# Ada units in rows of two, three and four between the weight units of a hybrid decoder layer

## Chip, core and metric

The kernel runs on one core of a Trainium2 chip. The time is device microseconds from launch to end; a run's profile also gives the span from the first to the last instruction. All times below are in microseconds unless a row says ns.

## What is computed

One decoder layer for 256 prompt rows and 8 x 4 sample rows (T = 288 rows together), model width 2048, feed-forward width 8192, all in float32:

```python
mod = jax.nn.silu(c) @ w_ada + b_ada            # 9 conditions, w_ada is 2048 x 12288
sh_m, sc_m, gt_m, sh_f, sc_f, gt_f = jnp.split(mod[:, None, :], 6, axis=-1)
h = rmsnorm(x, g_pre_mix) * (1 + sc_m) + sh_m
q, k, v, gu, gv = jnp.split(h @ w_in, SPLITS, axis=-1)
attn_out = attend(q, k, v)                       # sliding window, sinks, relative bias
gmlp_out, v_rows = gmlp_spatial_gate(jax.nn.gelu(gu), jax.nn.gelu(gv), ...)
merged = jnp.concatenate([rmsnorm(attn_out, g_attn_out), rmsnorm(gmlp_out, g_gmlp_out)], axis=-1)
x = x + gt_m * rmsnorm(merged @ w_out, g_post_mix)
h = rmsnorm(x, g_pre_ff) * (1 + sc_f) + sh_f
f = jnp.square(jax.nn.relu(h @ w_ff1)) @ w_ff2
x = x + gt_f * rmsnorm(f, g_post_ff)
```

## The kernel before

**Units.** Activations lie transposed: 16 tiles of 128 features by 288 rows. Weights come in units of 1 MB (128 x 2048 floats), loaded by SyncE's DMA queue into five buffers `raw`. A weight unit of W_out, f1 or f2 (class `Main`) yields 128 output features: its two halves are split into a rounded part `h` (cast on ScalarE, line 321) and a remainder `l` (subtraction on VectorE, line 322), and TensorE runs 48 matmuls of 288 columns (lines 336, 337, 340: h by xh, h by xl, l by xh). Then `evac` moves the sum out of PSUM.

An **Ada unit** (class `Ada`) is a quarter of a block of `w_ada` and is not split: four float32 matmuls of 512 columns (line 363; each stands as two instructions in the trace), whose weights are the 32 columns of `sc`, so each of the four fills another 32 columns of the array. Four units make a block. After the last, ScalarE copies the PSUM tile to an SBUF tile `adS` (line 367, two buffers). `ada_fin` then transposes it on TensorE (line 375, four transposes) and VectorE reduces and scales it into the modulation (lines 377 to 387). Blocks of kinds 2, 3 and 4 (`Gm`, `Bf`, `Af`; 48 units) are needed around the end of W_out and the start of f1, those of kind 5 (`Gf`; 16 units) only at the end of the last f2 pass.

**Stages, in order of time.** W_in with attention and gating; then W_out's first four output tiles in eight *slabs* of 0.5 MB (`SlabK`, line 924: each slab brings two of 16 feature tiles for four open PSUM tiles), among which stand the eight gates of the gating (lines 730 to 738), a sum over partitions (line 264) and the norm `rgate` that the last four slabs need; then W_out's other twelve output tiles as `Main` units (from 350 us); then `resid` (norm, residual add, second norm); f1's first six output tiles in eight slabs; and f1 and f2 in four passes of 16 and 16 units.

**What sets the order.** A list `items` is written by hand; `drive` walks it, loads four units ahead and splits one ahead. `na(n)` takes the next n Ada units, with a block's `ada_fin` as soon as its units are through. A tile scheduler then orders each engine's queue, with `high_priority` for the slabs, the attention pieces and `resid`; a queue is worked off in its order, so an instruction that waits holds up all that is behind it on its engine. Before, `NA_S` puts 1, 1, 1, 1, 1, 1, 2, 2 Ada units behind the eight slabs of W_out, `NA_O` one behind each W_out unit (two behind the last), eight (`NA_R`) stand behind `resid`, and f1 has one item of the list `adas2` (a unit or a block's transposes) behind each unit of its second pass and the start of its third. `gvout` (line 718) multiplies the gated rows by a gain on GpSimd for an output; it takes its tile from the two `adS` buffers.

Of the kernel before, what the change touches and what calls it, by code (L numbers as in the profile page):

```python
# [10 lines left out]
F32 = mybir.dt.float32  # L11
F32R = mybir.dt.float32r
AF = mybir.ActivationFunctionType
ALU = mybir.AluOpType
# [9 lines left out]
NS = NB * NT_S  # L24
T = NP + NS
# [3 lines left out]
NO = 4  # L29
# [16 lines left out]
NAFT = 4  # L46
NA_L = (0, 2, 1, 3, 3, 0, 2)
NA_A = (1, 1, 1, 1, 1, 1)
NA_O, NA_R = 13, 8
NA_S = (1, 1, 1, 1, 1, 1, 2, 2)  # L50

WID = {1: (1,), 2: (2,), 3: (1, 2), 4: (4,), 5: (1, 4), 6: (2, 4), 8: (4, 4)}

# [52 lines left out]
def build():  # L106
# [32 lines left out]
    with tile.TileContext(nc) as tc, ExitStack() as root:  # L139
        cp = root.enter_context(tc.tile_pool(name="cp", bufs=1))  # L140
# [5 lines left out]
        ap_ = mid.enter_context(tc.tile_pool(name="ap", bufs=1))  # L146
# [3 lines left out]
        V, S, PE, G = nc.vector, nc.scalar, nc.tensor, nc.gpsimd  # L150
# [148 lines left out]
        class Unit:  # L299
            src = None  # L300
            cols = 2 * HALF
            n = HALF
# [348 lines left out]
        gm = {}  # L651
# [65 lines left out]

        def gvout():
            for h in (0, 4):
                gr = cp.tile([128, 2, T], F32, name="adS", bufs=2).rearrange("p a b -> p (a b)")[:NS, :512]  # L720
                G.dma_start(gr, bass.AP(d_gain.tensor, h * 128, [[0, NS], [1, 512]]))
                G.tensor_tensor(gr, gr, gm["vGs"][:, h:h + 4].rearrange("p h c -> p (h c)"), ALU.mult)
                G.dma_start(o_g[:, h * 128:h * 128 + 512], gr)

        def gate(h):
# [31 lines left out]
        items = list(first)  # L757
# [38 lines left out]
        adas = []  # L796
# [3 lines left out]
        adas2 = []  # L800
# [4 lines left out]
        def na(n):  # L805
            out = []
            while adas and n > 0:
                it = adas.pop(0)
                out.append(it)
                n -= it.src is not None  # L810
            if adas and adas[0].src is None:
                out.append(adas.pop(0))
            return out
# [3 lines left out]
        def do(f, *a):  # L817
            def run():
                with tc.high_priority(offset=HP):
                    f(*a)  # L820
            items.append(Do(run))
# [108 lines left out]
        def slab_o(q):  # L930
            items.append(SlabK(d_woA[q], q, NO, pre_o, bo))
            items.extend(na(NA_S[q]))

        for q in range(4):
            slab_o(q)
            if q < 2:
                for h in range(4 * q, 4 * q + 4):
                    do(gate, h)
                    do(ssq_gate, h)
            if q == 2:  # L940
                do(rgate)
                do(gvout)
        for q in range(4, 8):
            slab_o(q)

        og = []

# [20 lines left out]
        def ev_bo():  # L968
            for n in range(NO):
                ev_o(n)(bo[n][:, :T])  # L970

        items.append(Do(ev_bo))
        for n in range(NO, 16):
            items.append(Main(d_woB[n - NO], xh, xl, ev_o(n)))
            items += na((n - NO + 1) * NA_O // (16 - NO) - (n - NO) * NA_O // (16 - NO))
        items += na(len([it for it in adas if it.src is not None]) - NA_R)

        def resid():
            r = norm_r(st["so"].result(), "r_o", 0.0)
# [66 lines left out]
        for c in range(4):  # L1046
            for j in range(16):
                if c == 0 and j < NF:
                    continue
                items.append(Main(d_f1B[c * 16 + j - NF], xh, xl, ev_f1(j)))  # L1050
                if c > 0 and adas2:
                    items.append(adas2.pop(0))
            for n in range(16):
                items.append(Main(d_f2[c, n], fh, fl, ev_f2(c, n)))

# [126 lines left out]
```

## Time and profile before

| | before |
|---|---|
| median of 3 runs (lowest, highest) | 1324.22 (1323.6, 1330.82) |
| the profiled execution | 1323.86 |
| its span, first to last instruction | 1322.1 |
| mean granted TensorE clock, share of full | 0.995 |
| TensorE matmul busy | 1291.5 (98%) |
| VectorE busy | 735.5 (56%) |
| ScalarE busy | 543.6 (41%) |
| GpSimd busy | 38.9 (3%) |
| DMA, mean over the span | 220 GB/s |

In the timeline rows the first number is the start, the second how long the engine is busy from the first start to the last end. Successive matmuls overlap, so what a piece of work costs is read from one start to the next, not from the busy time. A bracket names the idle time ahead of a row and what ended it.

### The profile page before, as it was taken

What the parts mean: (1) busy time and instruction counts of PE and PEld (TensorE: products, weight loads), DVE (VectorE), ACT (ScalarE), POOL (GpSimd) and SP (SyncE); (2) the same over time, 40 slices, a digit from 0 to 9 for tenths busy, and PEclk for the clock granted to TensorE, in tenths of its full rate; (3) what the DMA queues carried; (4) which work ended last, traced back from release to release, by engine and by line L of the source; (5) the groups of instructions that cost most, each with busy time, mean ns of one, the idle gap of its engine ahead of it and who ended that gap; (6) DMA issues with size and microseconds to landing.
All of it is one profiled execution on the core that took longest, in us unless ns stands there. A gap on an engine that the chain in (4) does not pass through costs nothing.

```text
span 1322.1 us, 23368 instructions
## 1 busy us (share of the span) xinstructions
PE 1291.5 (98%) x9770; PEld 1174.6 (89%) x9770; DVE 735.5 (56%) x1405; ACT 543.6 (41%) x873; POOL 38.9 (3%) x61
## 2 busy tenths in 40 slices
PE   6999999999999999999999999999999999999997
PEld 5789785767788699999998989999999999999996
DVE  5888676667744496543334444444554444555554
ACT  5323243575433265444344443334443334444331
POOL 0210001211000000000000000000000000000000
PEclk8999999999999999999999999999999999999999
DMA  9998977577987675544466765446444444454411
GB/s 357 337 325 313 334 284 249 204 278 255 384 319 258 275 271 189 177 169 161 160 223 239 268 234 187 171 171 232 166 176 165 160 160 164 169 178 160 159 65 72
DMA packets 46010, 291.40 MB, mean 220 GB/s; under 512 B 5834, under 2 KB 6410, under 8 KB 15056
## 3 DMA queue, kind: packets, MB, share of 16 engines
q1 hardware_dynamic: 43344, 284.26, 59.2%
q0 software_dynamic: 2416, 5.47, 1.8%
q8 instruction: 76, 1.25, 0.4%
q14 instruction: 30, 0.25, 0.0%
q10 hardware_dynamic: 144, 0.18, 0.0%
HBM read 287.18 MB, written 2.70 MB: 219 GB/s over the span
## 4 chain that ended last, share of the span: by engine, by line
PE 93%; DVE 4%; DMA 2%; ACT 1%; issue 0%; SPq 0%; DVEq 0%; ACTq 0%
PE ps L336 22%; PE ps L340 22%; PE ps L337 21%; PE ada L363 6%; PE ps L924 5%; PE ps L485 4%; PE ps L488 4%; PE ps L486 4%; PE ada L375 1%; DVE l L322 1%; PE ps L572 1%; DMA x<-xT 1%; PE ps L567 1%; DMA raw<-wada 1%; DMA raw<-win 0%; DVE acc L983 0%
## 5 line engine op out<-in xcount | busy, mean ns | idle before, releaser
L322 DVE TENSOR_TENSOR l<-raw,h 128x1024 fp32r<-128x1024 f32 (+3 forms) x368 | 417.6, 1141 | 345.7 <-ACT h L321 341.0
L321 ACT CAST h<-raw 128x1024 fp32r<-128x1024 f32 (+3 forms) x368 | 359.1, 984 | 571.0 <-PE ps L337 476.7
L336 PE MATMUL ps<-xh,h 128*128 128x288 f32 x1120 | 304.5, 299 | 0.9 <-ACT sq L1007 0.7
L337 PE MATMUL ps<-xl,h 128*128 128x288 f32 x1120 | 301.2, 295 | 0.0
L337 PE MATMUL ps<-fl,h 128*128 128x288 f32 x1024 | 276.9, 295 | 0.0
L336 PE MATMUL ps<-fh,h 128*128 128x288 f32 x1024 | 276.9, 298 | 0.0
L336 PEld LDWEIGHTS ps<-xh,h 128*128 128x128 f32 x1120 | 210.5, 188 | 23.8 <-ACT fh L1008 12.6
L337 PEld LDWEIGHTS ps<-xl,h 128*128 128x128 f32 x1120 | 211.6, 189 | 0.0
L336 PEld LDWEIGHTS ps<-fh,h 128*128 128x128 f32 x1024 | 193.0, 188 | 0.8 <-ACT fh L1008 0.8
L337 PEld LDWEIGHTS ps<-fl,h 128*128 128x128 f32 x1024 | 192.2, 188 | 0.0
L340 PE MATMUL ps<-xh,l 128*128 128x288 f32 x1120 | 171.9, 295 | 0.4 <-DVE l L322 0.4
L340 PE MATMUL ps<-fh,l 128*128 128x288 f32 x1024 | 157.3, 296 | 0.0
L340 PEld LDWEIGHTS ps<-xh,l 128*128 128x128 f32 x1120 | 156.1, 188 | 0.6 <-DVE l L322 0.6
L340 PEld LDWEIGHTS ps<-fh,l 128*128 128x128 f32 x1024 | 142.7, 188 | 0.0
L485 PE MATMUL ps<-xh,h 128*128 128x288 f32 x416 | 117.9, 307 | 2.9 <-DVE gv L497 2.0
L363 PE MATMUL ada<-raw,sc 128*32 128x512 f32 (+2 forms) x1088 | 109.1, 485 | 10.1 <-DMA raw<-wada 10.0
L486 PE MATMUL ps<-xl,h 128*128 128x288 f32 x416 | 117.2, 299 | 0.0
L485 PEld LDWEIGHTS ps<-xh,h 128*128 128x128 f32 x416 | 77.8, 190 | 17.2 <-issue 6.3
L488 PE MATMUL ps<-xh,l 128*128 128x288 f32 x416 | 86.7, 299 | 0.0
L486 PEld LDWEIGHTS ps<-xl,h 128*128 128x128 f32 x416 | 79.2, 191 | 2.6 <-issue 2.4
L488 PEld LDWEIGHTS ps<-xh,l 128*128 128x128 f32 x416 | 66.1, 190 | 1.1 <-issue 1.0
L363 PEld LDWEIGHTS ada<-raw,sc 128*32 128x32 f32 x1088 | 29.7, 113 | 39.5 <-issue 32.0
(255 smaller groups left out, 932.1 us busy)
## 6 DMA issues: line engine op xcount, KB each, us to landing
raw<-wada SPq DMA_DIRECT2D x96, 1024.0 KB, 6.8
raw<-f SPq DMA_DIRECT2D x64, 1024.0 KB, 4.8
raw<-f1B SPq DMA_DIRECT2D x58, 1024.0 KB, 4.8
raw<-woB SPq DMA_DIRECT2D x12, 1024.0 KB, 7.0
raw<-win SPq DMA_DIRECT2D x11, 1024.0 KB, 8.9
raw<-win SPq DMA_DIRECT2D x14, 640.0 KB, 5.1
raw<-f1A SPq DMA_DIRECT2D x8, 768.0 KB, 6.0
raw<-win SPq DMA_DIRECT2D x6, 768.0 KB, 5.9
```

Of the source, the lines that this page charges most:

```text
L321: S.copy(h, rw)
L322: V.tensor_tensor(l, rw, h.bitcast(F32), ALU.subtract)
L336: PE.matmul(ps, w, self.mh[:, k], start=k == 0, stop=False)
L337: PE.matmul(ps, w, self.ml[:, k], start=False, stop=False)
L340: PE.matmul(ps, l[:, kk * 128:kk * 128 + 128], self.mh[:, k], start=False, stop=k == 15)
L363: PE.matmul(ps[g:g + 32, :cw], sc[:, k], self.raws[:, kk * cw:kk * cw + cw], start=k < 4, stop=k >= KT - 4, skip_group_check=True)
L375: PE.transpose(pt[:, q * 128:q * 128 + 128], sb[:, q * 128:q * 128 + 128], ident)
L485: PE.matmul(ps, w, xh[:, k0 + kk], start=kk == 0, stop=False)
L486: PE.matmul(ps, w, xl[:, k0 + kk], start=False, stop=False)
L488: PE.matmul(ps, l[:, o_ + kk * 128:o_ + kk * 128 + 128], xh[:, k0 + kk], start=False, stop=kk == s - 1)
L567: PE.transpose(ps[:, to * 128:to * 128 + 128], L[:, hf, q * 128:q * 128 + 128], ident)
L924: PE.matmul(self.bk[n][:, :T], w[:, n * 128:n * 128 + 128], m[:, k], start=k == 0 and p_ == 0, stop=k == KT - 1 and p_ == 2)
```

## The change

Four things are done to the order of the work, and one to a tile.

- Slabs of W_out: Ada units 0, 2, 0, 2, 0, 2, 0, 2 behind the eight slabs, eight in all where there were ten.
- W_out's units: three Ada units behind every second one, fifteen in all where there were thirteen, and none behind the last one. Eight stay behind `resid`.
- f1: four Ada units behind the 4th, 8th, 12th and 16th unit of the second pass; the third pass has none.
- A new function `group` takes the units of a row; the transposes of a block that ends inside the row stand behind the row, those of a block that ends with the row stand behind the next row (`late`).
- `gvout` is asked for behind the sixth slab where it was behind the third, takes its tile from the buffers `bias`, and multiplies on VectorE.

```diff
-NA_O, NA_R = 13, 8
-NA_S = (1, 1, 1, 1, 1, 1, 2, 2)
+NA_O, NA_G = 3, 4
+NA_S = (0, 2, 0, 2, 0, 2, 0, 2)
...
-                gr = cp.tile([128, 2, T], F32, name="adS", bufs=2).rearrange("p a b -> p (a b)")[:NS, :512]
+                gr = ap_.tile([128, 2, 384], F32, name="bias", bufs=3).rearrange("p a b -> p (a b)")[:NS, :512]
                 G.dma_start(gr, bass.AP(d_gain.tensor, h * 128, [[0, NS], [1, 512]]))
-                G.tensor_tensor(gr, gr, gm["vGs"][:, h:h + 4].rearrange("p h c -> p (h c)"), ALU.mult)
+                V.tensor_tensor(gr, gr, gm["vGs"][:, h:h + 4].rearrange("p h c -> p (h c)"), ALU.mult)
...
+        late = []
+        def group(src, n):
+            out, ends = [], list(late)
+            late.clear()
+            while src and n:
+                it = src.pop(0)
+                if it.src is None:
+                    ends.append(it)
+                else:
+                    out.append(it)
+                    n -= 1
+            if src and src[0].src is None:
+                late.append(src.pop(0))
+            return out + ends
...
             items.append(Main(d_woB[n - NO], xh, xl, ev_o(n)))
-            items += na((n - NO + 1) * NA_O // (16 - NO) - (n - NO) * NA_O // (16 - NO))
-        items += na(len([it for it in adas if it.src is not None]) - NA_R)
+            if n % 2 and n < 15:
+                items += group(adas, NA_O)
+        items += late
+        late.clear()
...
                 items.append(Main(d_f1B[c * 16 + j - NF], xh, xl, ev_f1(j)))
-                if c > 0 and adas2:
-                    items.append(adas2.pop(0))
+                if c == 1 and j % NA_G == NA_G - 1:
+                    items += group(adas2, NA_G)
+                    if not adas2:
+                        items += group(adas2, 0)
```

What this makes of the queues is shown at three places. Names: `xh`, `xl` the two parts of the activations, `h`, `l` those of a weight unit, `raw` an unsplit unit, `ps` and `ada` PSUM tiles, `sqa` a sum of squares, `nr` and `mn` tiles of a norm, `gu` the gated rows.

TensorE in f1's second pass, the first Ada units of that pass, before:

```order
L337 MATMUL ps_7400<-xl_79,h_7336 128x288
L340 MATMUL ps_7400<-xh_78,l_7337 128x288 x8
L363 MATMUL ada_7465<-raw_7210,sc_95 32x512 x4
L336 MATMUL ps_7472<-xh_78,h_7392 128x288
L337 MATMUL ps_7472<-xl_79,h_7392 128x288
```

and now:

```order
L340 MATMUL ps_7587<-xh_78,l_7527 128x288 x8
L363 MATMUL ada_7652<-raw_7390,sc_95 32x512 x4
L363 MATMUL ada_7652<-raw_7455,sc_95 32x512 x4
L363 MATMUL ada_7652<-raw_7520,sc_95 32x512 x4
L363 MATMUL ada_7652<-raw_7585,sc_95 32x512 x4
L336 MATMUL ps_7687<-xh_78,h_7644 128x288
```

Four units of one block stand in a row where one stood. W_out's twelve units have five rows of three in the same manner, and one single unit inside the first of the twelve.

TensorE in W_out's slabs, around the sum over partitions that `rgate` needs, before:

```order
L924 MATMUL ps<-xh,h 128x288
L375 MATMUL ada<-small,adS 128x128 x4
L924 MATMUL ps<-xh,h 128x288 x3
L924 MATMUL ps<-xl,h 128x288 x2
L264 MATMUL ps<-sqa,ones_81 128x288
L924 MATMUL ps<-xl,h 128x288 x2
L924 MATMUL ps<-xh,l 128x288 x4
L363 MATMUL ada<-raw,sc 32x512 x12
L924 MATMUL ps<-xh,h 128x288 x4
```

and now:

```order
L924 MATMUL ps<-xl,h 128x288 x4
L363 MATMUL ada<-raw,sc 32x512
L924 MATMUL ps<-xh,l 128x288 x4
L264 MATMUL ps<-sqa,ones_81 128x288
L924 MATMUL ps<-xh,h 128x288 x4
L924 MATMUL ps<-xl,h 128x288 x4
L924 MATMUL ps<-xh,l 128x288 x4
L363 MATMUL ada<-raw,sc 32x512 x3
L375 MATMUL ada<-small,adS 128x128 x4
L363 MATMUL ada<-raw,sc 32x512 x8
L924 MATMUL ps<-xh,h 128x288 x4
```

The last row of each is the start of the fifth slab, which needs `rgate`. Between line 264 and it there were six slab matmuls and three units; now there are twelve slab matmuls, three quarters of a unit, a block's transposes and two units.

VectorE over the same norm, before:

```order
L224 TENSOR_SCALAR mn<-ps 128x288
L214 TENSOR_TENSOR mn<-nr 128x288
L215 SCALAR_TENSOR_TENSOR mn<-mn 128x288
L322 TENSOR_TENSOR l<-raw,h 128x512
L216 SCALAR_TENSOR_TENSOR nr<-mn,nr 128x288
L322 TENSOR_TENSOR l<-raw,h 128x512
L794 TENSOR_TENSOR nr<-nr 128x288
L891 SCALAR_TENSOR_TENSOR gu<-gu,small,nr 128x288 x3
```

and now:

```order
L722 TENSOR_TENSOR bias<-bias,vGs 32x512 x2
L322 TENSOR_TENSOR l<-raw,h 128x512
L224 TENSOR_SCALAR mn<-ps 128x288
L214 TENSOR_TENSOR mn<-nr 128x288
L322 TENSOR_TENSOR l<-raw,h 128x512
L215 SCALAR_TENSOR_TENSOR mn<-mn 128x288
L322 TENSOR_TENSOR l<-raw,h 128x512
L216 SCALAR_TENSOR_TENSOR nr<-mn,nr 128x288
L322 TENSOR_TENSOR l<-raw,h 128x512
L794 TENSOR_TENSOR nr<-nr 128x288
L377 TENSOR_REDUCE adm<-ada 128x36
L891 SCALAR_TENSOR_TENSOR gu<-gu,small,nr 128x288
```

Between line 214 and line 891 three subtractions and a block's reduction stand where two subtractions stood.

ScalarE in `resid`, from its first norm to the first tiles of f1, before:

```order
L166 ACTIVATE nr<-ps 128x288
L367 COPY adS<-ada 128x512
L166 ACTIVATE nr<-nr 128x288
L986 ACTIVATE adS<-x 128x576 x8
L367 COPY adS<-ada 128x512
L166 ACTIVATE nr<-ps,eps 128x288
L166 ACTIVATE nr<-nr 128x288
L321 CAST h<-raw 128x768
L291 ACTIVATE xh<-mn,mod_Bf 128x256 x2
L292 CAST xh<-mn 128x32
```

and now:

```order
L166 ACTIVATE nr<-ps 128x288
L166 ACTIVATE nr<-nr 128x288
L1006 ACTIVATE adS<-x 128x576 x8
L321 CAST h<-raw 128x768
L367 COPY adS<-ada 128x512
L166 ACTIVATE nr<-ps,eps 128x288
L321 CAST h<-raw 128x768
L166 ACTIVATE nr<-nr 128x288
L291 ACTIVATE xh<-mn,mod_Bf 128x256
L367 COPY adS<-ada 128x512
L291 ACTIVATE xh<-mn,mod_Bf 128x256
L292 CAST xh<-mn 128x32
```

The copy of a block has left the first norm; a cast has come into the second, and another block's copy between the first tile's two instructions.

## Rows read from the trace of the kernel before

**Rows 1.** The page, part 4: what the chain that ended last ran through.

```profile
PE 93%; DVE 4%; DMA 2%; ACT 1%; issue 0%; SPq 0%; DVEq 0%; ACTq 0%
```

**Rows 2.** Timeline of TensorE: start, us, engine, line, op, out<-in, count; f1 and f2.

```profile
569.81 0.29 PE L336 MATMUL ps<-fh,h 128*128 128x288 f32 x1
576.18 0.29 PE L336 MATMUL ps<-fh,h 128*128 128x288 f32 x1
...
686.18 1.06 PE L363 MATMUL ada<-raw,sc 128*32 128x512 f32 x8
687.18 0.40 PE L336 MATMUL ps<-xh,h 128*128 128x288 f32 x1
...
693.74 1.06 PE L363 MATMUL ada<-raw,sc 128*32 128x512 f32 x8
```

**Rows 3.** Timeline of TensorE: a block's transposes between two units of f1.

```profile
708.77 0.60 PE L375 MATMUL ada<-small,adS 128*128 128x128 f32 x4
709.13 0.38 PE L336 MATMUL ps<-xh,h 128*128 128x288 f32 x1
```

**Rows 4.** Timeline of TensorE: W_out's slabs from the partition sum to the first unit.

```profile
326.76 0.65 PE L264 MATMUL ps<-sqa,ones 128*128 128x288 f32 x2
...
331.46 1.07 PE L363 MATMUL ada<-raw,sc 128*32 128x512 f32 x8 [1.40 <-DMA raw<-wada]
332.50 0.80 PE L924 MATMUL ps<-xh,h 128*128 128x288 f32 x4
...
348.47 1.92 PE L363 MATMUL ada<-raw,sc 128*32 128x512 f32 x16
350.58 0.40 PE L336 MATMUL ps<-xh,h 128*128 128x288 f32 x1 [0.18 <-ACT h L321]
...
357.79 1.06 PE L363 MATMUL ada<-raw,sc 128*32 128x512 f32 x8
```

**Rows 5.** Timeline of ScalarE, the same stretch.

```profile
332.02 1.29 ACT L280 CAST xh<-gu 128x288 fp32r<-128x288 f32 x3 [2.57 <-DVE gu L891]
...
348.19 1.41 ACT L240 ACTIVATE sq<-ps 128x288 f32<-128x288 f32 x4 [3.95 <-PE ps L924]
349.49 1.98 ACT L321 CAST h<-raw 128x1024 fp32r<-128x1024 f32 x2
```

**Rows 6.** Timeline of VectorE, the same stretch.

```profile
330.38 0.68 DVE L322 TENSOR_TENSOR l<-raw,h 128x512 fp32r<-128x512 f32 x1
...
331.47 1.38 DVE L891 SCALAR_TENSOR_TENSOR gu<-gu,small,nr 128x288 f32<-128x288 f32 x3
```

**Rows 7.** Timeline of TensorE: from W_out's last unit into f1's slabs.

```profile
442.23 1.90 PE L363 MATMUL ada<-raw,sc 128*32 128x512 f32 x10
444.06 0.75 PE L264 MATMUL ps<-sqa,ones 128*128 128x288 f32 x2
...
461.94 3.64 PE L363 MATMUL ada<-raw,sc 128*32 128x512 f32 x32
466.10 1.06 PE L924 MATMUL ps<-xh,h 128*128 128x288 f32 x6 [0.52 <-ACT xh L292]
...
469.03 0.95 PE L924 MATMUL ps<-xh,h 128*128 128x288 f32 x6
```

**Rows 8.** Timeline of ScalarE, the same stretch.

```profile
444.85 0.41 ACT L166 ACTIVATE nr<-ps 128x288 f32<-128x288 f32 x1 [2.10 <-PE ps L264]
445.86 0.59 ACT L367 COPY adS<-ada 128x512 f32<-128x512 f32 x1 [0.60 <-PE ada L363]
446.35 0.45 ACT L166 ACTIVATE nr<-nr 128x288 f32<-128x288 f32 x1
...
462.49 0.82 ACT L321 CAST h<-raw 128x768 fp32r<-128x768 f32 x1
```

**Rows 9.** Windows: stretch, length, engines' busy time, granted clock, DMA share, GB/s.

```profile
350.00:360.00 10.00, 9.44 (x69) 7.81 (x66) 7.74 (x15) 4.79 (x7) 0.00 (x0) 1.00 1.02 422
390.00:400.00 10.00, 10.00 (x77) 9.00 (x77) 6.19 (x9) 3.86 (x6) 0.00 (x0) 1.00 0.72 242
```

More of the change, by code (lines that the diff above doesn't have):

```diff
@@ L941, in build @@
                 do(rgate)
-                do(gvout)
         for q in range(4, 8):
             slab_o(q)
+            if q == 5:
+                do(gvout)
         og = []
```

## Prediction

> **What bounds the kernel now.** I read the chain of waits first: 93% of it is TensorE and 4% VectorE [rows 1]. So a microsecond counts where TensorE's queue gets shorter, except where another engine holds it. Next, the timeline of TensorE in f1, for the price of an Ada unit. Two weight units that follow each other start 576.18 - 569.81 = 6.37 apart [rows 2]. With an Ada unit between them, the Ada unit stands for 687.18 - 686.18 = 1.00, and the weight unit ahead of the next one takes 693.74 - 687.18 = 6.56 [rows 2]. The 0.19 more is the wait on the way into the Ada unit. A single Ada unit costs 1.19. Then rows of Ada units: one is busy for 1.06 [rows 2], two for 1.92 [rows 4], four for 3.64 [rows 7]. Each that joins adds 0.86. So a row of n costs 1.19 + 0.86 (n - 1), and each unit that joins a row saves 0.33. Last, the two places where TensorE waits for a chain on ScalarE and VectorE: the norm ahead of the fifth slab of W_out [rows 4 to 6], and `resid` [rows 7, 8].
>
> **f1: -4.0.** Sixteen singles cost 16 x 1.19 = 19.0. Four rows of four cost 4 x (1.19 + 3 x 0.86) = 15.1. That is 3.9 to 4.0 saved, all on TensorE, which here waits for nothing else. The four blocks' transposes stay: one costs 0.36 [rows 3] and about 0.09 on the way in. Three now stand behind the next row, where that entry is gone; the last one needs ScalarE's copy, 0.59 long [rows 8], while one transposition and two matmuls cover it. I take 0 for them together, between -0.3 and +0.7 (a copy stuck behind one cast of a weight unit, half of the 1.98 in [rows 5]). Weights: the four units of a row have each a buffer that a weight unit left one or two units earlier, so they have landed before the row. The second weight unit behind a row takes the buffer of the first, and its load stands in SyncE's queue until that one is split, with the two loads behind it. The row and the first unit, 3.8 + 6.4 long, cover it; without that cover it would cost one landing per row.
>
> **W_out's units: +2.4.** Between the twelve units stood eleven singles, 11 x 1.19 = 13.1. Now there are one single and five rows of three, 1.19 + 5 x (1.19 + 2 x 0.86) = 15.7, because two units came from the slabs and two from behind the last unit. That is +2.6, and +0.4 for one block's transposes more. The first unit took 357.79 - 350.58 = 7.21 [rows 4], 0.65 over the 6.56, for its split came late. Now transposes and an Ada unit stand inside it, behind eleven of its matmuls, and give the split that time: -0.65.
>
> **The slabs: -2.1.** Three steps. (a) *To the partition sum*, 326.76 before [rows 4]. TensorE has ahead of it one Ada unit less, six slab matmuls less (0.13 each, 6.37 / 48) and one block's transposes less: 1.2 + 0.8 + 0.4 = 2.4. The gates need rows that ScalarE and GpSimd finish at the same time as before, so TensorE, there earlier, waits for them: I take -2.0, between -1.0 and -2.4. (b) *From the sum to the fifth slab.* Before, 332.50 - 326.76 = 5.74. The DMA wait of 1.40 in the row of Ada units ahead of it [rows 4] is not what held it: the first cast of the gated rows starts at 332.02 [rows 5] and the slab starts as it ends. So the chain of the norm sets this start, and relief on the DMA alone gives nothing. That chain gets longer: on VectorE one 128x512 subtraction more (0.68 long, 0.60 to the next [rows 6]) and a block's reduction, on ScalarE one cast between the two steps of the norm (about 0.55, the subtraction's counterpart). I take +1.3, so the slab starts 0.7 earlier; bounds: 0 (all of it in idle slots) and +2.2 (the reduction waits for transposes that wait for ScalarE's copy). `gvout`'s two multiplications on VectorE stand just ahead of this chain; the partition sum and the first ScalarE step cover them, and I take 0 (up to +1.2 if they come late, twice a subtraction). GpSimd's part of `gvout` released nobody. (c) *Fifth to eighth slab.* Before, two singles with a block's transposes between them, 1.2 + 0.4 + 1.0; now one single: -1.4. The first unit of W_out then waits for four squares and a cast on ScalarE, 348.19 to 349.49 and half of 1.98 [rows 5]; this held it at 350.58, 2.11 after the last slab [rows 4], though two Ada units filled 1.85 of it. One fills it now, so nothing is gained there: 0. Sum -2.0 + 1.3 - 1.4 = -2.1 (from -3.6 to +0.1).
>
> **`resid`: -1.1.** It began at 442.23 with Ada units; the partition sum started at 444.06, behind one and a quarter of them [rows 7]. Now a block's transposes and a quarter stand there: 0.4 earlier. In the norm, ScalarE did the first step at 444.85 and then waited for a block's copy, so that the second came at 446.35, 1.05 after the first could have let it go [rows 8]. That copy is gone: -1.05. In the second norm a cast now stands between the two steps: 0.82 long [rows 8], and the subtraction of its half stands on VectorE ahead of the next step. A copy of 0.59 stands between the first tile's instructions. I take +1.35 for these three, between +0.6 (casts alone, the rest beside) and +2.4 (all in series). The first slab is relieved in turn: transposes of 0.4 leave it, and its first eighteen matmuls, 469.03 - 466.10 = 2.93 where 18 x 0.13 = 2.4 would do [rows 7], find their splits ready: -0.9. Sum -0.4 - 1.05 + 1.35 - 0.9 = -1.0 to -1.1 (from -2.3 to +0.5). The eight units behind it stay in its shadow.
>
> **DMA in W_out.** A row of three and two units takes 2 x 6.37 + 2.91 = 15.65 and five loads of 1.05 MB. At 422 GB/s (350 to 360) a load takes 2.5 and five 12.4; at the poorest busy stretch, 242 GB/s at a share of 0.72, a full queue would give 336 GB/s, 3.1 a load, 15.6 in all [rows 9]. So the loads just fit, and I take 0. The Trainium skill speaks against such rows: "DMA: Bandwidth & Descriptors", "Where 436 GB/s comes from", holds that loads from HBM are bound near 358 GB/s per core. This trace shows more, 422 in the window above. By the page, an estimate of 2.93 a load, five would take 14.6, so the sum would be the same and the slack 1.0 instead of 3.2.
>
> **Sum.** -4.0 + 2.4 - 2.1 - 1.1 = -4.8 on the profiled execution's 1323.86: 1319.1. That execution lies 0.4 below the median of the runs, 1324.22; I give 1319.1.
>
> **Rivals.** *The chains do not lengthen.* Casts and subtractions put between the norms' steps fall into idle time. For: both engines wait much around 332 and 462 [rows 5, 6, 8]. Against: in the queues they stand between steps that wait for each other. Then (b) is 0 and the +1.35 is +0.6: 1319.1 - 1.3 - 0.75 = 1317.0, and with the f1 transposes at their best 1316.7. *The chains eat the gain outside f1.* Bounds of slabs and `resid` at their worst together would be -4.0 + 2.4 + 0.1 + 0.5, or 1322.9; half way, 1321.0. For: ScalarE's copies stand in front of both chains. Against: they would all have to come late. *Slower than before: the rows of three become bound by the DMA.* From 3.13 a load (15.65 / 5) TensorE waits in each row; with 25 loads in five rows the 4.8 are used up from 3.13 + 4.8 / 25 = 3.32 a load, 316 GB/s. At 3.5 it would be 1319.1 + 25 x 0.37 = 1328.4. For: the window of 242 GB/s at 0.72 comes near. Against: 422 GB/s just before, when the queue was full. *The change does not do what it says*: in W_out's slabs the scheduler already undid pairs (the order shows units alone there); this is in the sum. In f1 and W_out's units the rows stand as asked.
>
> **How the numbers follow.** Forecast 1319.1 with its own range 1317.7 to 1321: 0.50. Chains not longer, 1315.5 to 1317.7: 0.25. Chains worse, 1321 to 1323: 0.20. DMA, 1324 to 1330: 0.05. The range 1315.8 to 1322.6 leaves out the last and the ends of the two before, under 0.2. What a measurement of this kernel can tell from no change is about 0.5%, 6.6: faster means below 1317.6. That takes in the first rival and a tail of the forecast: 0.28. Slower, above 1330.8, only the far end of the DMA case: 0.03. Same: 0.69.
>
> **What would show it.** In the profile after, an Ada row of four in f1 from start to the next weight unit 3.6, of three in W_out 2.7; if a row is longer, with a DMA named as the releaser, the DMA rival holds. The fifth slab should start near 331.8 and 7 behind the partition sum, the first W_out unit near 348.5, W_out's last unit end near 442.5, f1's first slab near 466 with ScalarE's cast named ahead of it; the norm's second step in `resid` should follow its first at once. I am wrong if f1's second pass is shorter by anything but 4, or if the slabs give back more than they lose.

## The result and the profile after

| | before | after |
|---|---|---|
| median of the runs compared (lowest, highest) | 1326.36 of 7 (1323.6, 1330.82) | 1317.53 of 7 (1317.09, 1320.14) |
| ratio after to before, 95% interval | | 0.9943 [0.9931, 0.9955] |
| the profiled execution | 1323.86 | 1320.14 |
| its span | 1322.1 | 1318.4 |
| first matmul of W_out's slabs | 301.74 | 303.92 |
| from there to the sum over partitions at the end | 1003.84 | 997.94 |

The ratio is taken over undisturbed executions alone, so it is not the quotient of the two medians. It says 0.57% faster, 0.45 to 0.69%. The last two rows say how to read it. All that the change touches lies behind the first matmul of W_out's slabs, and there the trace of after is 5.9 shorter. Ahead of it the engines of both kernels work off the same instructions in the same order, but for the order of the last few loads that SyncE asks for (from 293.65 on in before), and there this execution of after happened to be 2.2 later. The waits of TensorE between 300 and 510 (who waits <- for whom: us in total, times, longest):

```profile
PE ps L245 <- ACT adS L1006: 3.2, 4, 1.7
PE ada L375 <- ACT adS L367: 1.9, 3, 0.8
...
```

No wait for a DMA is left, in the lines left out neither; before, 1.40 were put down to one [rows 4]. What is there is waits for ScalarE, but for one of 0.6 for GpSimd's rows, at the gates of the first slabs. TensorE in f1 (start, us, engine, line, op, out<-in), a row of four, against [rows 2]:

```profile
698.24 3.64 PE L363 MATMUL ada<-raw,sc 128*32 128x512 f32 x32
701.81 0.40 PE L336 MATMUL ps<-xh,h 128*128 128x288 f32 x1
...
727.46 3.64 PE L363 MATMUL ada<-raw,sc 128*32 128x512 f32 x32
...
757.06 3.64 PE L363 MATMUL ada<-raw,sc 128*32 128x512 f32 x32
```

Four units stand for 3.57. The second row starts 29.22 behind the first, with four weight units between; the third 29.60 behind the second, with a block's transposes besides. In W_out's slabs, against [rows 4]:

```profile
327.05 0.65 PE L264 MATMUL ps<-sqa,ones 128*128 128x288 f32 x2
...
330.96 0.66 PE L375 MATMUL ada<-small,adS 128*128 128x128 f32 x4 [0.70 <-ACT adS L367]
331.55 1.92 PE L363 MATMUL ada<-raw,sc 128*32 128x512 f32 x16
333.65 0.80 PE L924 MATMUL ps<-xh,h 128*128 128x288 f32 x4 [0.18 <-ACT xh L280]
...
349.90 0.40 PE L336 MATMUL ps<-xh,h 128*128 128x288 f32 x1 [1.04 <-ACT h L321]
```

The DMA wait of 1.40 has become a wait of 0.70 for a block's copy and one of 0.18 for the gated rows. So the norm's chain comes last at the fifth slab by 0.18 only; before, the slab started right behind an Ada unit, without idle time [rows 4]. The first W_out unit, with one Ada unit ahead of it where two stood, waits 1.04 where it waited 0.18: nothing gained, as forecast. VectorE over that norm, against [rows 6]:

```profile
329.12 0.46 DVE L214 TENSOR_TENSOR mn<-nr 128x288 f32<-128x288 f32 x1 [0.39 <-ACT nr L166]
329.50 0.68 DVE L322 TENSOR_TENSOR l<-raw,h 128x512 fp32r<-128x512 f32 x1
330.10 0.45 DVE L215 SCALAR_TENSOR_TENSOR mn<-mn 128x288 f32<-128x288 f32 x1
...
332.41 0.30 DVE L377 TENSOR_REDUCE adm<-ada 128x36 f32<-128x144 f32 x1
332.63 0.50 DVE L891 SCALAR_TENSOR_TENSOR gu<-gu,small,nr 128x288 f32<-128x288 f32 x1
```

Every second instruction belongs to somebody else, in the lines left out too: three subtractions of 0.6 and a reduction of 0.2 between the norm's own steps. In `resid`, TensorE and ScalarE, against [rows 7, 8]:

```profile
445.25 0.75 PE L264 MATMUL ps<-sqa,ones 128*128 128x288 f32 x2
...
451.30 2.21 PE L245 MATMUL ps<-adS,ones 128*128 128x288 f32 x8 [1.73 <-ACT adS L1006]
...
467.03 0.66 PE L375 MATMUL ada<-small,adS 128*128 128x128 f32 x4 [0.78 <-ACT adS L367]
467.54 1.07 PE L924 MATMUL ps<-xh,h 128*128 128x288 f32 x6
```

```profile
446.04 0.41 ACT L166 ACTIVATE nr<-ps 128x288 f32<-128x288 f32 x1 [1.69 <-PE ps L264]
446.49 0.44 ACT L166 ACTIVATE nr<-nr 128x288 f32<-128x288 f32 x1
...
461.87 0.51 ACT L166 ACTIVATE nr<-ps,eps 128x288 f32<-128x288 f32 x1
462.26 0.83 ACT L321 CAST h<-raw 128x768 fp32r<-128x768 f32 x1
462.99 0.45 ACT L166 ACTIVATE nr<-nr 128x288 f32<-128x288 f32 x1
...
466.41 0.56 ACT L367 COPY adS<-ada 128x512 f32<-128x512 f32 x1
```

The first norm's two steps follow each other at once. In the second one the cast stands between them, and the last block's copy stands ahead of the first tile's second instruction.

Windows of W_out (columns as in [rows 9]):

```profile
370.00:380.00 10.00, 10.00 (x77) 9.93 (x75) 2.19 (x5) 0.41 (x1) 0.00 (x0) 1.00 0.95 401
400.00:410.00 10.00, 10.00 (x78) 10.00 (x77) 3.69 (x7) 1.30 (x2) 0.00 (x0) 1.00 1.01 426
```

TensorE is busy without a gap while the queue brings 401 to 426 GB/s: the rows of three do not wait for their loads.

### The profile page after: what moved, and what is told of

Same layout as the page of the kernel before. It is cut to its first block, busy times and chain, and to the rows that moved or that the text cites. A ratio compares the mean times of both kernels' runs of the same rounds, so it can differ in the third digit from the quotient of the medians.

```text
span 1318.4 us, 23358 instructions
## 1 busy us (share of the span) xinstructions
PE 1286.0 (98%) x9770; PEld 1177.8 (89%) x9770; DVE 735.3 (56%) x1407; ACT 540.0 (41%) x873; POOL 36.1 (3%) x59
## 4 chain that ended last, share of the span: by engine, by line
PE 60%; DVE 1%; ACT 0%; DVEq 0%; issue 0%
PE ps L336 20%; PE ps L340 20%; PE ps L337 19%; PE ada L363 1%; DVE acc L1086 0%; DVE x L1092 0%; PE ada L375 0%; PE ps L1083 0%; ACT nr L166 0%; PE ps L270 0%; PE ps L264 0%; DVE mn L214 0%; DVE mn L215 0%; DVE nr L216 0%; DVE mn L224 0%; DVEq L139 0%
## 5 line engine op out<-in xcount | busy, mean ns | idle before, releaser
L363 PE MATMUL ada<-raw,sc 128*32 128x512 f32 (+2 forms) x1088 | 104.4, 480 | 7.4 <-DMA raw<-wada 7.4
```

What stands on the lines that cost most here:

```text
L363: PE.matmul(ps[g:g + 32, :cw], sc[:, k], self.raws[:, kk * cw:kk * cw + cw], start=k < 4, stop=k >= KT - 4, skip_group_check=True)
```

## The experiments

All traces cut at the same six starts on TensorE: first slab matmul of W_out, its first `Main` unit, `resid`'s partition sum, first slab of f1, first `Main` unit of f1, the last partition sum. The first column is where the cut begins, the others are lengths.

| kernel | first slab at | slabs | units to the sum | resid | f1 slabs | f1 and f2 | from the first slab |
|---|---|---|---|---|---|---|---|
| before | 301.74 | 48.84 | 93.48 | 22.04 | 40.00 | 799.48 | 1003.84 |
| e5_before (before again) | 301.46 | 48.83 | 93.50 | 22.03 | 40.00 | 799.48 | 1003.85 |
| e1_f1_rows | 300.65 | 48.82 | 93.48 | 22.03 | 40.01 | 795.22 | 999.54 |
| e6_f1_rows (the same) | 305.50 | 48.86 | 93.49 | 22.04 | 40.01 | 795.08 | 999.48 |
| e12_f1_rows (the same) | 301.75 | 48.84 | 93.49 | 22.04 | 40.00 | 795.27 | 999.64 |
| after | 303.92 | 45.98 | 95.35 | 22.29 | 39.08 | 795.23 | 997.94 |
| e3_again (after again) | 302.07 | 45.97 | 95.34 | 22.07 | 39.09 | 795.23 | 997.70 |
| e2_rest | 303.55 | 45.97 | 95.35 | 22.07 | 39.09 | 799.48 | 1001.95 |
| e4_gvout | 301.42 | 45.70 | 95.36 | 22.07 | 39.09 | 795.27 | 997.48 |
| e7_dense | 303.62 | 45.98 | 100.64 | 21.50 | 39.07 | 795.23 | 1002.42 |
| e8_own_row | 301.40 | 45.98 | 96.22 | 22.10 | 39.07 | 795.84 | 999.21 |
| e9_norm | 302.35 | 45.68 | 95.35 | 20.35 | 39.84 | 795.26 | 996.48 |
| e10_f1_two | 306.29 | 45.97 | 95.34 | 22.08 | 39.08 | 796.31 | 998.78 |
| e11_f1_eight | 307.47 | 45.98 | 95.32 | 22.09 | 39.08 | 812.99 | 1015.46 |

One kernel repeats itself from the first slab on within 0.24, and most stages within 0.05, while the start of the first slab moves by nearly 7. So a single trace settles a question of half a microsecond behind the first slab, and none ahead of it.

**Two halves.** The rows in f1 alone:

```diff
-                if c > 0 and adas2:
-                    items.append(adas2.pop(0))
+                if c == 1 and j % NA_G == NA_G - 1:
+                    items += group(adas2, NA_G)
+                    if not adas2:
+                        items += group(adas2, 0)
```

> The kernel before, with the rows of four in f1 alone; everything ahead of f1 as before. By the price of an Ada unit (1.19 alone, 0.86 for each that joins a row) the second pass gets 4.0 us shorter, so the time is 4.0 to 4.3 below the kernel before, and the stretch from the first f1 unit to the last partition sum 795.2 to 795.5 where before had 799.5. If the rows only hide a wait that comes back elsewhere in f1 or f2, it is nearer 0 to 2. If the kernel as changed owes its whole gain of about 7.5 to f1, this one is 7 below.

The other half is the changed kernel with this edit undone:

> The changed kernel with f1 as before: single Ada units behind the units of the second pass. What is left is W_out's slabs, W_out's units, the tile and engine of gvout, and the chains of resid. The sum of the prediction gives +2.4 - 2.1 - 1.1 = -0.8 against the kernel before; the two traces, read from the first slab to f1's first unit, give -1.7. If the part of the gain that neither accounts for (about 1.6) sits outside f1 and is real, this is near -3.3; if it was the disturbance of single executions in the first 60 us, -0.8 to -1.7.

And the changed kernel beside them:

> The changed kernel itself once more, beside the two halves on the same chip. If the two halves add up, its gain is the sum of theirs: about 5.0 to 6.0 by the traces from the first slab on. If the gain of 7.5 of the first comparison is real in full, it shows 7 to 8 again.

Measured, against the kernel before at a median of 1325.7 in 23 runs: f1 rows 1321.93, ratio 0.9971 [0.9959, 0.9983]; the rest 1322.29, 0.9971 [0.9953, 0.9988]; both 1318.02, 0.9944 [0.9932, 0.9957]. From the first slab on, the f1 rows give -4.3, the rest -1.9, both -6.1: they add up, and f1 holds two thirds. The rest is 1.1 better than the prediction's -0.8 and agrees with the traces. Its time is 3.4 below before by the medians, so 1.5 more than its own stages show: that lies ahead of the first slab, in runs of both kernels.

**gvout back in its place.**

```diff
-                gr = ap_.tile([128, 2, 384], F32, name="bias", bufs=3)...
+                gr = cp.tile([128, 2, T], F32, name="adS", bufs=2)...
-                V.tensor_tensor(gr, gr, ...)
+                G.tensor_tensor(gr, gr, ...)
...
+                do(gvout)        # behind the third slab, no more behind the sixth
```

> The changed kernel with gvout as before: asked for behind the third slab, in a tile of the two adS buffers, multiplied on GpSimd. The prediction costed gvout at nothing: then the time is that of the changed kernel within 0.5 us, and the fifth slab starts as in it. If the loan of an adS buffer holds up a block's copy and its transposes in the slabs, 0.5 to 2 us slower than the changed kernel. If VectorE's two multiplications ahead of the norm cost something, up to 0.9 faster.

Measured 1317.75, 0.9949 [0.9933, 0.9964], and 997.48 from the first slab: 0.22 shorter than the changed kernel, with 0.27 less in the slabs. The cost of nothing was right within 0.3, and the sign is on the side of the old place. The norm's chain is not where the 0.27 comes from. The fifth slab does start 0.21 earlier, but the stretch behind it is 0.34 longer. What gains is the first W_out unit, which starts 1.93 behind the last slab matmul where it was 2.33: ScalarE's queue now has three squares ahead of its cast and the fourth behind it.

**Where executions differ.** The kernel before and the f1 rows once more, for traces:

> The kernel before itself, for another trace. Among 23 timed runs its span has a median 2.4 above its lowest, where 18 runs of the kernels with the new W_out lie only 0.9 above theirs (by median); from the first slab to the last partition sum the traces give 1003.84 before and 997.5 to 997.9 with the change. If the wider spread arises ahead of the first slab, which the change does not touch, this trace again has 1003.8 from the first slab on, and the first slab starts anywhere from 300.6 to 304. If the old slabs or the old W_out units lose time in some executions, the stretch from the first slab to f1's first unit, 204.36 in the first trace, is 1 to 3 longer here, with a wait that the first trace did not have.

> The kernel before with the rows of four in f1 alone, for another trace of the old slabs and W_out units: in 12 timed runs its span had a median 3.5 above its lowest, and the trace taken was the lowest. If the spread arises ahead of the first slab, the stretch from the first slab to f1's first unit is 204.3 again; if in the old slabs or W_out, 1 to 4 longer, with a wait or a stretch of low granted clock that names the place.

Measured: both have the stretch of their first traces to 0.1, 1003.85 and 999.48. So neither old slabs nor old units lost time in these executions. The second one started its first slab at 305.50. A window of that trace, the same window of e1_f1_rows, and the wait ahead of it in both, in this order:

```profile
225.00:230.00 5.00, 5.00 (x25) 2.62 (x25) 0.28 (x1) 0.96 (x2) 1.02 (x2) 0.50 0.31 127
225.00:230.00 5.00, 5.00 (x38) 2.53 (x34) 1.53 (x4) 0.77 (x2) 1.41 (x2) 1.00 0.74 192
```

```profile
221.24 0.66 PE L376 MATMUL ada<-small,adS 128*128 128x128 f32 x4 [2.03 <-ACT adS L368]
221.08 0.66 PE L376 MATMUL ada<-small,adS 128*128 128x128 f32 x4 [2.02 <-ACT adS L368]
```

TensorE waits 2.03 for a copy, some matmuls later the granted clock is 0.50, the 1.2 GHz level, and the engine is busy all the time at half speed. In e1_f1_rows the same wait of 2.02 stands at the same place, and the clock stays at 1.00: the wait alone does not decide it. In the trace of after the clock fell at another place, to a mean of 0.66 between 55 and 60.

The Trainium skill, "TensorE: Matmul & The Clock Gate", "What's actually happening", names two levels of the clock and says that the point at which it changes varies from run to run of one kernel. These traces agree: 0.50 or 1.00 at the same place in the same queue.

How long the clock was at half ahead of the first slab nearly orders the first column of the table. It was never at half in e1_f1_rows (first slab at 300.65). It was so for about 3 in e5_before, e4_gvout, e8_own_row and e9_norm (301.40 to 302.35), for about 7 in before, e12_f1_rows, after, e3_again, e2_rest and e7_dense (301.74 to 303.92), and for 10 to 17 in e6_f1_rows, e10_f1_two and e11_f1_eight (305.50 to 307.47). Where the stretches are alike, old and new slabs start alike: 301.46 in e5_before and 301.42 in e4_gvout; 301.74 in before and 302.07 in e3_again.

The f1 rows were run once more, last of the kernels that were run in turn:

> The kernel before with the rows of four in f1 alone, once more, now run last of its round; in the first comparison it ran right behind the kernel before. From the first slab to the last partition sum it has 999.5. Ahead of the first slab all kernels work off the same queues, yet the first slab started at a median of 303.7 and 304.2 in the runs of the two kernels with the old W_out, and at 301.4 to 302.2 in those of the four with the new one. If that hangs on the place in the round, its median is now 301.5 to 302.5, and its time 1319.2 to 1320; if it is a property of the kernel, 303.5 to 304.5, and 1321.5 to 1322.5.

Measured 1320.51, 0.9965 [0.9947, 0.9983]. A run's span less its kernel's fixed rest gives the start of its first slab. Medians: before 303.65 in 23 runs and 303.75 in 17; f1 rows 304.2 in 12 and now 302.65 in 12; the kernels with the new slabs 301.4, 302.1, 302.2, 302.1 and 302.2 (after, e3_again, e2_rest, e4_gvout and e9_norm, in 7, 5, 11, 6 and 6 runs). The second value of the f1 rows lies between the two expectations, so the place in the round is not shown to be the cause, nor is the kernel: single runs with the new slabs started at 306.29 and 307.47. The granted clock goes some of the way. Its mean is 0.9956 and 0.9952 in the two sets of before, 0.9961 and 0.9959 in the two of the f1 rows, and 0.9960 to 0.9969 in the kernels with the new slabs, and 0.001 of the span is 1.3. Why it was granted less to before, and what the rest of the 1.6 is, stays open.

**The price of a row.** Rows of two and of eight in f1:

```diff
-NA_O, NA_G = 3, 4
+NA_O, NA_G = 3, 2      # the other one: 3, 8
```

> The changed kernel with rows of two in f1 behind every second unit of the second pass, in place of rows of four behind every fourth: eight units join a row where twelve did. At 0.33 for each, the stretch from the first f1 unit to the last partition sum, 795.23 with rows of four and 799.48 with singles, is 795.23 + 4 x 0.33 = 796.5. If most of the gain of the rows came from the transposes that stand behind the next row, it is nearer 795.5; if only from rows that are long, nearer 798.5.

> The changed kernel with two rows of eight in f1 in place of four rows of four: fourteen units join where twelve did. By the price alone the stretch from the first f1 unit to the last partition sum is 795.23 - 2 x 0.33 = 794.6. But five buffers hold the first five units of a row; the sixth is loaded once the first is through, some 5 later, and each behind it 2.5 later, while TensorE takes 0.86 for a unit. By the theory that buffers and loads bound the length of a row, TensorE waits 1.2 to 1.6 at each of the last three units and 2 to 3 at the weight unit behind: 6 to 7 a row, and the stretch is 806 to 809.

Rows of two (time 1323.33, one run): 796.31, 0.2 from the price. Rows of eight (1341.19, one run): 812.99, 17.8 longer than rows of four, and more than expected. TensorE in the first of its two rows, and a window behind:

```profile
726.99 4.50 PE L363 MATMUL ada<-raw,sc 128*32 128x512 f32 x40
731.42 0.66 PE L375 MATMUL ada<-small,adS 128*128 128x128 f32 x4
732.96 1.07 PE L363 MATMUL ada<-raw,sc 128*32 128x512 f32 x8 [0.89 <-DMA raw<-wada]
735.42 1.06 PE L363 MATMUL ada<-raw,sc 128*32 128x512 f32 x8 [1.40 <-DMA raw<-wada]
739.13 1.28 PE L363 MATMUL ada<-raw,sc 128*32 128x512 f32 x8 [2.64 <-DMA raw<-wada]
742.68 0.61 PE L336 MATMUL ps<-xh,h 128*128 128x288 f32 x1 [2.27 <-ACT h L321]
```

```profile
740.00:745.00 5.00, 2.73 (x13) 2.32 (x10) 2.34 (x2) 3.44 (x4) 0.00 (x0) 0.50 1.02 428
```

Five units run through, which is what the five buffers hold; the sixth, seventh, eighth and the next weight unit wait 0.89 + 1.40 + 2.64 + 2.27 = 7.2, as the theory of the buffers has it. What it did not have is the last line: behind these waits the clock is granted at half, and the next matmuls pay for it. With the transposes between the units this makes up the rest of the 17.8 / 2 = 8.9 a row, as far as the trace tells.

**Loads in W_out.** The five rows of three behind the first five units:

```diff
-            if n % 2 and n < 15:
+            if n < NO + 5:
```

> The changed kernel with its five rows of three behind the first five of W_out's units, one behind each, so that a unit and a row (6.37 + 2.91 = 9.3) stand against four loads of 1.05 MB, 2.3 each. The loads of the changed kernel landed 2.45 to 2.5 apart in a full queue. If that is what a load takes, each row falls 0.5 to 0.7 behind, 2 to 3.5 in all less what the five buffers hold at the start (about one load, 2.5): TensorE waits in or behind the last rows and the time is 0 to 3 above the changed kernel. By the Trainium skill, DMA: Bandwidth & Descriptors, Where 436 GB/s comes from, bound near 358 GB/s, an estimate of 2.93 a load: 4 x 2.93 - 9.3 = 2.4 a row, 10 to 12 in all. If TensorE sees no wait at all, the same as the changed kernel within 0.5.

Measured 1324.3, and 1002.42 from the first slab, 4.7 more than the changed kernel: 5.3 more in W_out's units, 0.6 less in `resid`. TensorE behind the first, second and fourth row, and ScalarE behind the first two:

```profile
362.23 0.40 PE L336 MATMUL ps<-xh,h 128*128 128x288 f32 x1 [1.65 <-ACT h L321]
...
372.20 0.39 PE L336 MATMUL ps<-xh,h 128*128 128x288 f32 x1
...
392.64 0.40 PE L336 MATMUL ps<-xh,h 128*128 128x288 f32 x1 [0.45 <-ACT h L321]
```

```profile
360.65 0.59 ACT L367 COPY adS<-ada 128x512 f32<-128x512 f32 x1 [2.33 <-PE ada L363]
361.13 2.00 ACT L321 CAST h<-raw 128x1024 fp32r<-128x1024 f32 x2
...
370.14 1.99 ACT L321 CAST h<-raw 128x1024 fp32r<-128x1024 f32 x2 [0.79 <-DMA raw<-woB]
```

Little of this is waiting for loads. The longest wait, 1.65, is for a cast whose weight unit had landed at 358.38; in ScalarE's queue the copy of the row's block stands ahead of that cast, and the copy waited 2.33 for TensorE to end the row. The cast that did wait for its load (370.14) held up nobody: the unit behind it starts at 372.20 without idle time. One wait is a load's by the trace, the 0.45: that unit landed at 391.46 and its cast began at 391.54. Behind the fifth row 0.76 went to a copy, which waited for the row's end, and 0.29 to a cast behind that copy. The rest is TensorE's own work: transposes break up two rows (0.3 each), and ahead of the partition sum stand one and a quarter Ada units where the changed kernel has a quarter (0.86). So the 4.7 lies above the expected 0 to 3, and waiting for loads is 0.45 of it by the trace, 1.5 if the fifth row is put down to them as well.

The loads did come slower than I had set. Fifteen landed between 360.81 and 401.92, 41.1 / 15 = 2.74 each, 383 GB/s, where I had 2.5; at least two were under way all the time. The estimate from the 358 GB/s of the Trainium skill, "DMA: Bandwidth & Descriptors", "Where 436 GB/s comes from" (2.93 a load, 10 to 12 in all) is too high on both counts. The section "Measured" of the same page of the Trainium skill gives 425 GB/s for large transfers of a core alone, which the fullest windows reach (426 above).

**Transposes behind their own row.**

```diff
             if src and src[0].src is None:
-                late.append(src.pop(0))
+                ends.append(src.pop(0))
```

> The changed kernel with the transposes of a block that ends with a row asked for directly behind that row, in place of behind the next row: they need ScalarE's copy of 0.59 at once. If TensorE has to wait for that copy, each of these blocks (four in f1, some in W_out) costs 0.5 to 0.8 and one entry of 0.09 more, 2.5 to 5 in all. If the scheduler puts matmuls of the next unit ahead of the transposes, they cost an entry into and out of their kind each, and the whole is 0 to 1 above the changed kernel, so that the new place of the transposes gave next to nothing.

Measured 1318.91, and 999.21 from the first slab, 1.5 more: 0.87 in W_out's units and 0.61 in f1. The scheduler put two to nineteen matmuls ahead of the transposes. In f1 those of one block waited all the same; TensorE, and ScalarE ahead of it:

```profile
701.68 0.66 PE L375 MATMUL ada<-small,adS 128*128 128x128 f32 x4 [0.54 <-ACT adS L367]
```

```profile
699.15 2.00 ACT L321 CAST h<-raw 128x1024 fp32r<-128x1024 f32 x2 [1.92 <-DMA raw<-f1B]
701.05 0.58 ACT L367 COPY adS<-ada 128x512 f32<-128x512 f32 x1
```

The block's copy stood behind the cast of a weight unit, the case for which the prediction had set aside up to 0.7. The other blocks cost no more than before: from the second row to the third and from the third to the fourth it is 29.62 and 29.60, and in the changed kernel, where a block's transposes stand directly behind the row, 29.60 both times. The 0.87 in W_out is not the transposes' either. As many of them, and as many rows, stand ahead of the partition sum as in the changed kernel, but one and a quarter Ada units just ahead of it where there was a quarter: 0.86. So the second expectation holds for the transposes themselves: their new place gave next to nothing. The 1.5 are one late copy and one Ada unit that moved.

**The chain of resid.** The second half's cast and subtraction of f1's first slab behind the norm and the first tile, the second tile behind the first, the last block's copy behind the first tile (with gvout as before):

```diff
-                    S.copy(h, rw)
-                    V.tensor_tensor(l, rw, h.bitcast(F32), ALU.subtract)
+                    behind(S.copy(h, rw).ins, [order["now"][-1]] if c0 and first_f1_slab else [])
+                    behind(V.tensor_tensor(l, rw, h.bitcast(F32), ALU.subtract).ins, [st["sm"]] if c0 and first_f1_slab else [])
...
-                    S.copy(sb[:, :cw], ps[:, :cw])
+                    behind(S.copy(sb[:, :cw], ps[:, :cw]).ins, [st["sc"]] if self.blk == (3, 12, 4) else [])
...
-            V.scalar_tensor_tensor(t[:, :NP], x[:, k, :NP], ...)
+            behind(V.scalar_tensor_tensor(t[:, :NP], x[:, k, :NP], ...).ins, [st["sm"]] if k == 1 and B is mods["Bf"] else [])
...
-        items.append(Do(resid_hi))
+        items += [Do(resid_hi), Do(pre_hi)]
```

`first_f1_slab` stands for the test on the unit. Here `behind` fixes an order on one engine; `order["now"][-1]` is the norm's last step on ScalarE, `sm` and `sc` are the first tile's last product and cast, and `pre_hi` asks for the first tile right behind `resid` (the slab then leaves it out; that line is not shown).

> The changed kernel with gvout as before, and with the second norm of resid cleared: the second half's cast of f1's first slab behind the norm's last step on ScalarE, its subtraction behind the first tile's products on VectorE, the products of the second tile behind those of the first, and the last block's copy behind the first tile. In the changed kernel the subtraction of 0.96 alone puts off the norm's first product from 460.65 to 461.92 and the copy and the second tile's products put off the first tile's small cast by 0.8. By the theory that this chain sets the start of f1's first slab, the stretch from resid's partition sum to that slab, 22.07, gets 1.3 to 1.8 shorter (the Ada row ahead of it ends 1.7 before the slab now), and the eight slabs, 38.14, get 0.3 to 0.9 longer, since their first split comes later: from the first slab to the last partition sum 996.3 to 997.1, after 997.48 with the chain as it is. If the slab waits for something else, 997.5 as before; if VectorE has no room for the subtraction between the tiles, 998.

Measured 1316.95, 0.9935 [0.9923, 0.9947], and 996.48 from the first slab: `resid` 1.72 shorter than in e4_gvout, the slabs 0.75 longer, both inside what was expected. About 0.5 of the 1.72 is a block's transposes, which moved from ahead of the slab to behind its first six matmuls; the net gain is 1.0. ScalarE, VectorE and TensorE:

```profile
460.32 0.44 ACT L166 ACTIVATE nr<-nr 128x288 f32<-128x288 f32 x1
460.67 0.82 ACT L321 CAST h<-raw 128x768 fp32r<-128x768 f32 x1
```

```profile
460.91 0.45 DVE L214 TENSOR_TENSOR mn<-nr 128x288 f32<-128x288 f32 x1
```

```profile
460.12 3.64 PE L363 MATMUL ada<-raw,sc 128*32 128x512 f32 x32
463.73 1.06 PE L924 MATMUL ps<-xh,h 128*128 128x288 f32 x6
464.89 0.66 PE L375 MATMUL ada<-small,adS 128*128 128x128 f32 x4
```

The norm's steps follow each other, and the slab now starts on the heels of the Ada row: the row has taken the chain's place as what ends last, so this place has no more to give by a shorter chain. This is the best of the kernels by its trace, 1.2 below the changed kernel's 997.70; by the timed runs alone the two can't be told apart.

## Why the prediction was right or wrong

The time, 1317.53, lies in the range (1315.8 to 1322.6) and 1.6 below the forecast of 1319.1: just below the forecast's own bracket (from 1317.7 on), in the one that I gave to the first rival. The class that I held likeliest, within 0.5%, is left by 0.07 of a per cent, with 0.5% inside the interval. By the stages, predicted and measured (before less e3_again, or after where it differs):

| step | predicted | measured |
|---|---|---|
| f1 | -4.0 | -4.25 |
| W_out's units, with the 0.4 of `resid`'s sum | +2.0 | +1.86 |
| slabs (a), to the partition sum | -2.0 | -1.9 |
| slabs (b), sum to fifth slab | +1.3 | +0.87 |
| slabs (c), fifth to eighth slab | -1.4 | -1.85 |
| slabs, last slab matmul to the first unit | 0 | 0 |
| `resid`, from its sum to f1's first slab | -1.05 + 1.35 | +0.03 (+0.25 in after) |
| f1's slabs | -0.9 | -0.91 |
| sum | -4.7 | -6.1 (-5.9) |

**f1**: right, and 0.25 more than forecast. A row of four cost less than I had: from the start of one to the start of the next it is 29.22 in the changed kernel where no transposes stand between, less four weight units of 6.37 leaves 3.74, where the price gave 3.77. A block's transposes cost 29.60 - 29.22 = 0.38, where I had 0.36 + 0.09. I took 0 for them, between -0.3 and +0.7. Three of them behind rows give -0.2, the four rows -0.1. That they stand behind a row is not shown to be the reason, since between matmuls they cost 0.38 to 0.40 in e8_own_row. The price (0.33 for a unit that joins) held for rows of two, three and four, where it comes out at 0.37, 0.34 and 0.34.

**W_out's units**: right, by the price and without any wait behind the first unit. The loads' cover was thinner than I had it: 2.5 a load held in this kernel, but a queue kept full for 41 us ran at 2.74 (e7_dense). With 3.13 a load as the point where rows wait, the slack was 0.39 a load and not 0.63.

**Slabs**: the step whose sizes were off, by 0.8 in all. (a) was right with its mechanism: the work of 2.4 is gone, and TensorE now waits 0.6 for GpSimd's rows at the gates. In (b) I added the cast, the subtraction and the reduction in full, 0.55 + 0.6 + 0.2. The cast was partly covered: from the sum to the norm's first product it is 329.12 - 327.05 = 2.07, 0.37 more than before. From there to the first gated row it is 332.63 - 329.12 = 3.51, 0.50 more, for two of VectorE's own steps had taken 0.1 to 0.2 longer to the next one than they do with a stranger behind them. In (c) I gave -1.4 for the transposes and the Ada unit that left. TensorE in the slabs behind the fifth one's start, before and now:

```profile
333.90 0.70 PE L924 MATMUL ps<-xh,l 128*128 128x288 f32 x4
...
343.47 0.80 PE L924 MATMUL ps<-xh,h 128*128 128x288 f32 x4
...
346.27 0.70 PE L924 MATMUL ps<-xh,l 128*128 128x288 f32 x4
```

```profile
334.85 0.69 PE L924 MATMUL ps<-xh,l 128*128 128x288 f32 x4
...
341.24 0.80 PE L924 MATMUL ps<-xh,h 128*128 128x288 f32 x4
...
342.41 0.70 PE L924 MATMUL ps<-xh,l 128*128 128x288 f32 x4
```

The eight matmuls around the pair took 346.27 - 343.47 = 2.80 before, and the eight behind the one Ada unit that is left take 342.41 - 341.24 = 1.17 now. So the pair cost 1.63: next to each other and inside a slab they cost more than my prices for each. The other 0.2 is the fifth slab's start. Its first eight matmuls took 333.90 - 332.50 = 1.40 before and take 334.85 - 333.65 = 1.20 now: a slab that starts later finds its tiles further on. The same shows in e1_f1_rows, where (b) was 0.19 longer and (c) 0.20 shorter than in e12_f1_rows (5.92 and 15.56 against 5.73 and 15.76), and in e4_gvout, 0.21 shorter and 0.34 longer than in the changed kernel. So (b) and (c) had to be priced as one stretch; together I gave -0.1, and they gave -1.0.

**resid**: right in each of its parts. The first norm lost its copy: from the sum to the last group of line 245 it is 1.15 shorter (15.31 before, 14.16 in e3_again), against 1.05. The second norm got 1.2 to 1.4 longer from that group to the slab (6.73 before, 7.91 and 8.13), against 1.35. e9_norm confirms the mechanism: with the strangers out of the chain 1.0 of this comes back.

**The rivals**: the time is next to that of the first one (1316.7 to 1317.0), the chains that do not lengthen, but that rival did not happen: both chains got longer, by 0.87 and 1.2 to 1.4. The stages went 1.4 beyond the forecast, about 0.45 each in (b) and (c) and 0.25 each in f1 and `resid`, nearly all errors on one side: that the time came so near the rival's is luck. For the ratio the part ahead of the first slab comes on top. That part is the rest of the ratio: 0.57% of 1326 are 7.5, the stages give 6.0, and 1.5 lie where the change does nothing. By the stages alone the ratio would be 1 - 6.1 / 1326 = 0.9954, inside the interval at its upper end, and within 0.5% as forecast. The lowest runs of the two kernels agree with that: 1323.31 and 1317.09, 6.2 apart.

## What to carry to other kernels

Price a change of order from one start to the next of the engine that is bound, and cut the traces at a start behind which they repeat: here most stages repeat to 0.05 while whole runs spread by 7. Work that a scheduler puts between the steps of a waiting chain costs less than its length where the chain has gaps, and a late start is partly caught up behind it, so price the chain and what it starts as one stretch. Where a wait names an engine, read what stood ahead of the releaser in its queue: a cast of a weight unit was late behind a block's copy, and a copy behind a cast, with their own inputs long there. A row of units pays as long as the buffers hold it; each unit beyond them costs a load, and the clock may fall behind the wait.

## What the runs showed of the hardware that I had not expected

- Half the clock at different places of the same queue: 0.50 between 225 and 230 in e6_f1_rows and 1.00 in e1_f1_rows, behind the same wait of 2.0; 0.66 between 55 and 60 in after. Four of the fourteen traces had a stretch at half around 225, in three of them about 10 long, and these three have the first slab at 305.5 to 307.5, all others at 300.7 to 303.9.
- Behind a row that waits for loads the clock falls too (0.50 between 740 and 745 in e11_f1_eight), so that a wait costs more than its length.
- A queue that always has at least two loads of 1.05 MB under way lands one in 2.74 over 41 us, 383 GB/s (e7_dense), with windows of 5 us between 324 and 428 GB/s.
